# A hybrid encoder layer on one core: selection a block behind its queries, a deeper weight ring for the first tile, smaller gate blocks

## The chip, the core and the metric

The kernel runs on one core of a Trainium2 chip. TensorE (PE) multiplies, VectorE (DVE) and ScalarE (ACT) do elementwise work, GpSimd (POOL) issues the indirect DMAs that gather rows by index, and SyncE (SP) issues nearly all other DMAs, in the order in which they stand in its program. Every engine runs its own instructions in order; what is behind a waiting instruction waits too. The metric is the time of one execution in device microseconds.

## What is computed

One layer over 512 tokens of width 2048, all in float32: a normed projection, retention and dilated attention ("mixers"), their merge into the residual stream, and a product-key expert layer (PEER). The last part of the reference, which the change touches, is

```python
merged = sigmoid(gate_ret) * ret + sigmoid(gate_att) * att
x = x + merged @ w_out[l]
h2 = rms_norm(x, ffn_norm_g[l])
q = (h2 @ w_query).reshape(B, S, 8, 256)              # 8 heads
s1 = einsum('bshd,hkd->bshk', q[..., :128], sub_keys[:, 0])   # 128 keys each
s2 = einsum('bshd,hkd->bshk', q[..., 128:], sub_keys[:, 1])
v1, i1 = top_k(s1, 16); v2, i2 = top_k(s2, 16)
best, pos = top_k(v1[..., :, None] + v2[..., None, :], 16)    # over 256 pairs
experts = e1 * 128 + e2;  gates = softmax(best)
a   = gelu(h2 . u[experts]) * gates                   # 16384 experts, 8 x 16 per token
out = x + sum(a * v[experts])
```

## The kernel before

The 512 tokens are four tiles of 128. Tile 0 goes through the whole front alone, then tiles 1 to 3 together; the functions `mixers`, `merge` and `routing` are called once for each of these two stages (T = 1 and T = 3).

Every weight matrix comes through `load_w`: 512 KB pieces (`wraw`) are loaded by SP, ACT rounds each to `whi`, DVE takes the rest as `wlo` (L131), and PE uses both (L146 to L148). These buffers are a ring, opened by `weight_pool(raw, parts)`: raw pieces and parts that can be held at a time. It is (4, 4) from the start to the end of tile 0's routing, (3, 2) in the second `mixers`, (4, 3) in the second `merge` and `routing`.

`merge` multiplies by `w_ret_out` and `w_attn_out`, then `w_out`; the sum with x is kept in `x1`, stored to DRAM (`x1D`), squared for the norm on ACT (into `xr`), scaled in place by its norm and transposed. `routing` runs over four blocks c of 512 query columns: it multiplies (8 pieces of `w_query`), transposes the queries (L648) and multiplies with the keys `skT` (L653); then DVE picks the top 16 of all scores (L520 to L524, L668 to L710), 114 instructions for one block at T = 3. The keys come as 4 DMAs and are transposed on PE (L724). In the first stage four gemms of gates (`fillers`) run beside the four query gemms.

Tiles 0 and 1 get their experts by gathers: 256 each, one 1 MB row set for every (token column, expert) of u and then of v, issued by POOL (L756) and used on DVE (L765 for u, L774 for v). `tick(anchor, rate)` hangs `rate` gathers on a DVE instruction of other work. Tiles 2 and 3 get theirs densely: `expert_in(n)` multiplies the tokens with u of 128 experts (48 matmuls of 256 columns, L854 to L856; two `ur` loads, two `uh` on ACT, two `ul` on DVE), and `expert_out(g, i)` multiplies the gated results with v (L980 to L982, two loads `vr`, two `vl` on DVE). Their gates lie in a table in DRAM, `GD`, that is made in between: for 8 tokens at a time (an iteration; 32 of them) DVE makes one-hot rows (L912, L913, L922), ACT scales them (L920), PE multiplies them (L924), ACT copies the result to `Gs` (L926); a finished block of `Gs` (TB = 64 tokens, 4 MB) is stored to `GD`.

The order in the second stage: `routing` calls `begin_dense` behind its last query block, which runs the first NFIRST = 11 `expert_in`; behind the selection its results are transposed (hkT), written to DRAM and read back; then the 32 iterations with 12 more `expert_in` and one gather each; then the dense loop: 16 groups of 8 `expert_out` steps. The first three groups tick 0.7 gathers a step (`early_rate`), and two of them have no `expert_in` beside them; the gathers that are left are spread over the 96 steps of the next twelve groups. The program order on each engine is not that of the source: a scheduler places the instructions.

Of the kernel before, what the change touches and what calls it, by code (L numbers as in the profile page):

```python
# [10 lines left out]
F32 = mybir.dt.float32  # L11
BF16 = mybir.dt.bfloat16
F32R = mybir.dt.float32r
U32 = mybir.dt.uint32
I32 = mybir.dt.int32
AF = mybir.ActivationFunctionType
ALU = mybir.AluOpType
AX = mybir.AxisListType

P = 128  # L20
# [6 lines left out]
H = 8  # L27
# [37 lines left out]
def hybrid_layer(ctx, tc, I, out, dbg=None):  # L65
    nc = tc.nc
# [33 lines left out]
    ident = const.tile([P, P], F32, name="ident")  # L100
# [3 lines left out]
    def bank(name, pool=None):  # L104
        return (pool or psB).tile([P, 512], F32, name=name, tag="bank")
# [49 lines left out]
    with tc.tile_pool(name="x0", bufs=1) as x0:  # L155
# [22 lines left out]
        for k in range(KT):  # L178
            ps = bank("xT")
# [360 lines left out]
    def merge(part, mg, pieces):  # L540
# [63 lines left out]
        for c in range(4):  # L604
            cs = slice(c * 512, (c + 1) * 512)
            ps = gemm((I["w_out"][0], c * 512, tiles(mT)))[0]
            for t in range(T):
                xr = mg.tile([P, 512], F32, name="xr", tag="xr", bufs=3)
                nc.sync.dma_start(xr, x4[t0 + t][:, cs])
                nc.vector.tensor_add(x1[t][:, cs], ps[t], xr)  # L610
                nc.sync.dma_start(x1D[t0 + t][:, cs], x1[t][:, cs])
                nc.scalar.activation(xr, x1[t][:, cs], AF.Square, accum_out=ss4[:, t, c:c + 1])
        fg = mg.tile([P, KT], F32, name="ffng")
        nc.sync.dma_start(fg, I["ffn_norm_g"][0].rearrange("(k p) -> p k", p=P))
        for t in range(T):
# [17 lines left out]
    def routing(T, rt, skT, tab, tiles2, before_last=None):  # L633

        N2 = 2 * T
        gates, e1, e2 = [rt.tile([P, T, 8, 16], F32, name=n, bufs=1) for n in ("gates", "e1", "e2")]
        for c in range(4):
            ps = paired((I["peer_w_query"][0], c * 512, tiles2))
            qn = rt.tile([P, T, 512], F32, name="qn", bufs=2)
            for t in range(T):  # L640
                nc.scalar.copy(qn[:, t], ps[t])
            v12 = rt.tile([P, T, 2, 2, 16], F32, name="v12")
            i12 = rt.tile([P, T, 2, 2, 16], U32, name="i12")
            scs = []
            for i in range(4):
                pt = bank("qT")
                for t in range(T):
                    nc.tensor.transpose(pt[:, t * P:(t + 1) * P], qn[:, t, i * P:(i + 1) * P], ident)  # L648
                qT = rt.tile([P, T * P], F32, name="qTs", bufs=2)
                nc.scalar.copy(qT, pt[:, :T * P])  # L650
                ss = bank("s12")
                for t in range(T):
                    nc.tensor.matmul(ss[:, t * P:(t + 1) * P], qT[:, t * P:(t + 1) * P], skT[:, 4 * c + i],  # L653
                                     start=True, stop=True)
                sc = rt.tile([P, T * P], F32, name="s12s", bufs=4)
                nc.scalar.copy(sc, ss[:, :T * P])
                scs.append(sc)
            if c == 3 and before_last:
                before_last()
            for i in range(4):  # L660
                for t in range(T):
                    scr = rt.tile([P, P], F32, name="scr")
# [14 lines left out]
            for a in range(N2):  # L677
# [32 lines left out]
            nc.vector.tensor_mul(gates.rearrange("p t (c u) k -> p t c u k", c=4)[:, :, c],  # L710
                                 ex.rearrange("p (t u) k -> p t u k", t=T),
                                 sm.rearrange("p (t u) -> p t u", t=T)[:, :, :, None].to_broadcast([P, T, 2, 16]))
        return e1, e2, gates

    def routing_tables(rt):
        tab = rt.tile([P, 3, 16], F32, name="tab", bufs=1)
        nc.sync.dma_start(tab.rearrange("p a b -> p (a b)"), bcast(I["c_rank"], 48))
        skT = rt.tile([P, 16, P], F32, name="skT", bufs=1)
        for q4 in range(4):
            sk = rt.tile([P, 4, P], F32, name="sk", bufs=1)  # L720
            nc.sync.dma_start(sk, I["peer_sub_keys"][0].rearrange("h s k d -> k (h s) d")[:, 4 * q4:4 * q4 + 4])
            ps = bank("skT")
            for i in range(4):
                nc.tensor.transpose(ps[:, i * P:(i + 1) * P], sk[:, i], ident)  # L724
            nc.scalar.copy(skT[:, 4 * q4:4 * q4 + 4].rearrange("p a b -> p (a b)"), ps)
        return skT, tab


# [6 lines left out]
    def unit(t, e1, e2, gates, h2row):  # L735

        u = Unit()
        u.t = t
        u.eid = ga.tile([P, P], I32, name=f"eid{t}")
        u.gate = ga.tile([P, P], F32, name=f"gate{t}")  # L740
        ef = ga.tile([P, P], F32, name="ef", tag="ef")
        nc.vector.scalar_tensor_tensor(ef, flat(e1), float(P), flat(e2), op0=ALU.mult, op1=ALU.add)
        nc.vector.tensor_copy(u.eid, ef)  # L743
        nc.vector.tensor_copy(u.gate, flat(gates))
        u.h2 = h2row
        gstate["todo"] += [(u, s) for s in range(2 * P)]
        return u
# [40 lines left out]
    h2gD = dram.tile([P, D], F32, name="h2gD")  # L788
    mixers(0, True)
    wk_ctx.close()  # L790
    ga = ctx.enter_context(tc.tile_pool(name="ga", bufs=1, reuse_waits="tile"))
    with tc.tile_pool(name="mgA", bufs=1, reuse_waits="tile") as mg, \
            tc.tile_pool(name="rtA", bufs=2, reuse_waits="tile") as rt, \
            tc.tile_pool(name="flA", bufs=2, reuse_waits="tile") as fl:
# [11 lines left out]
        unit(0, e1[:, 0], e2[:, 0], gates[:, 0], h2gD)  # L806


    weight_pool(3, 2)
    mode["tick"] = lambda a: tick(a, 0.85)  # L810
    mixers(1, False)
# [2 lines left out]

    TG = 2
    ND = TG * P
    TB = 64
    NB = ND // TB
    NE = 2
    NV = 8  # L820
    NGRP = P // NV
    NPRE = 24
    NFIRST = 11
    NLAST = 1
    right = ctx.enter_context(ExitStack())
    pools = {}
# [68 lines left out]
    with tc.tile_pool(name="gb", bufs=1, reuse_waits="tile") as gb:  # L895
# [6 lines left out]
        for blk in range(NB):  # L902
            for n in range(*[NFIRST + (NPRE - NLAST - NFIRST) * (blk + i) // NB for i in (0, 1)]):
                expert_in(n)
            Gs = gb.tile([P, P, TB], F32, name="Gs")
            for o in range(TB // OB):
                t0 = blk * TB + o * OB
                cols = lambda v: v[:, t0:t0 + OB, None].to_broadcast([P, OB, P])
# [5 lines left out]
                for q in range(OB // 4):  # L914
# [9 lines left out]
                        nc.tensor.matmul(ps[:, i * P:(i + 1) * P], oh2[:, j], oh1[:, j], start=True, stop=True)  # L924
                    j0 = o * OB + 4 * q
                    nc.scalar.copy(Gs[:, :, j0:j0 + 4], ps.rearrange("p (t e) -> p e t", t=4))  # L926
                tick(last, 1.0)
            nc.sync.dma_start(GD[blk], Gs)
        for n in range(NPRE - NLAST, NPRE):
            expert_in(n)  # L930
# [7 lines left out]

    W = {}

    def gate_tile(m):
        Gt = d2.tile([P, NB, NE * TB], F32, name="Gt")
        nc.sync.dma_start(Gt, GD[:, :, NE * m:NE * (m + 1), :].rearrange("b p e t -> p b (e t)"))
        return Gt

    def weigh(m, Gt):
        ge = A_out.pop(m)
        gv = ge.rearrange("p j (b t) -> p b j t", t=TB)
        nc.vector.tensor_mul(gv, gv, Gt.rearrange("p b (j t) -> p b j t", t=TB))
        wh = d2.tile([P, NE, ND], F32R, name="wh", bufs=7)  # L950
        wl = d2.tile([P, NE, ND], F32R, name="wl", bufs=7)
        nc.scalar.copy(wh, ge)
        nc.vector.tensor_sub(wl, ge, wh.bitcast(F32))
        W[m] = (wh, wl)

    G0 = NPRE // NV
    early_rate = 0.7
    left_steps = [(NGRP - 1 - G0) * 8]

    def expert_out(g, i):  # L960
# [36 lines left out]
    for g in range(NGRP + 1):  # L997
        for q in range(NV):
            n = NV * g + q
            if n < P:  # L1000
                if n % NE == 0:
                    Gt = gate_tile(n // NE)
                if n >= NPRE:
                    expert_in(n)
                if n % NE == NE - 1:
                    weigh(n // NE, Gt)
            if g > 0:
                expert_out(g - 1, q)
# [8 lines left out]
def laid_out(inputs):  # L1017
    host = {n: np.ascontiguousarray(inputs[n]) for n in _INS}
    u = host["peer_u"].reshape(P, P, KT, P)
    host["u_feat"] = np.ascontiguousarray(u.transpose(0, 3, 2, 1)).reshape(P, P, KT * P)  # L1020
    host.update(shape_constants())
    return host

# [16 lines left out]
```

## Time and profile before

| | us |
|---|---|
| median of 3 runs | 4591.96 (4589.6 to 4595.62) |
| the profiled execution | 4602.08 |
| its span, first to last instruction | 4600.3 |
| PE busy in the span | 4211.8 (92%) |
| DVE busy | 3439.3 (75%) |
| ACT busy | 1917.0 (42%) |

The profiled execution is 10 us above the median, and 2 us of it lie outside its span. Busy PE time holds waits for weights inside a group of matmuls only in part, so a stage is read by its window: how long it lasts, how much of it PE and DVE are busy, which clock TensorE was granted (1.00 is full), and the share of the 16 DMA engines that was in use.

### The profile page before, as it was taken

The numbers are of one execution on the slowest core, as the hardware profiler recorded it, in microseconds if no ns is written. First come the engines' busy times: TensorE is split into PE (matmuls) and PEld (weight loads), VectorE is DVE, ScalarE is ACT, GpSimd is POOL, SyncE is SP. The second block draws the span as 40 slices with busy tenths as digits, with TensorE's granted clock in tenths as the row PEclk, the third lists the DMA queues.
The fourth block names the chain that finished last, engine by engine and source line by source line (L and its number), as shares of the span: only waits on it lengthen the run. The fifth ranks groups of instructions, "written<-read, shape, count | busy, mean of one in ns | idle before, by whom it ended". The sixth has DMA issues, their size and how long they took to land.

```text
span 4600.3 us, 57918 instructions
## 1 busy us (share of the span) xinstructions
PE 4211.8 (92%) x21638; PEld 3524.4 (77%) x21638; DVE 3439.3 (75%) x4495; ACT 1917.0 (42%) x2674; POOL 795.5 (17%) x516
## 2 busy tenths in 40 slices
PE   8999998988998999989979977886799999999999
PEld 6878776765776778767758866786689998899997
DVE  7454554546566878677678878888779998999997
ACT  6444555545442323443432333344434443344443
POOL 0000000000002112222122221012112332344332
PEclk9999999999999999999989998998899999999999
DMA  7666675758658889888899885267889999999997
GB/s 241 226 219 218 215 243 178 244 193 287 224 160 303 323 290 331 313 305 320 300 346 373 340 323 202 92 236 292 318 302 363 397 400 391 401 400 402 405 403 293
DMA packets 510171, 1358.78 MB, mean 295 GB/s; under 512 B 49216, under 2 KB 129088, under 8 KB 440768
## 3 DMA queue, kind: packets, MB, share of 16 engines
q1 hardware_dynamic: 432800, 816.00, 50.9%
q0 software_dynamic: 73728, 536.90, 29.7%
q8 instruction: 170, 2.79, 0.2%
q10 hardware_dynamic: 3360, 2.17, 0.2%
q14 instruction: 113, 0.93, 0.1%
HBM read 1290.05 MB, written 64.88 MB: 295 GB/s over the span
## 4 chain that ended last, share of the span: by engine, by line
PE 50%; DMA 18%; DVE 13%; issue 13%; ACT 3%; POOL 2%; SPq 0%; ACTq 0%; DVEq 0%; POOLq 0%
PE gB L147 9%; PE gB L148 9%; PE gB L146 9%; PE psy L981 3%; PE psy L982 3%; PE psy L980 3%; PE psa L856 3%; PE psa L854 3%; PE psa L855 3%; DMA gr<-in_peer_v,eid 3%; DMA ur<-in_u_feat 3%; DMA wraw<-in_w_in 2%; POOL gr L756 2%; DVE wlo L131 2%; DMA vr<-in_peer_v 2%
## 5 line engine op out<-in xcount | busy, mean ns | idle before, releaser
L131 DVE TENSOR_TENSOR wlo<-wraw,whi 128x1024 fp32r<-128x1024 f32 x752 | 917.2, 1223 | 650.6 <-ACT whi L130 636.0
L130 ACT CAST whi<-wraw 128x1024 fp32r<-128x1024 f32 x752 | 789.4, 1051 | 1227.7 <-PE gB L148 913.6
L756 POOL DMA_INDIRECT gr<-in_peer_u,eid x256 | 362.9, 1418 | 2752.8 <-DVE eid L743 1535.1
L774 DVE SCALAR_TENSOR_TENSOR accg<-gr,wg,accg 128x2048 f32<-128x2048 f32 x256 | 600.5, 2346 | 50.6 <-DMA gr<-in_peer_v,eid 38.5
L765 DVE SCALAR_TENSOR_TENSOR gr<-gr,hrow 128x2048 f32<-128x2048 f32 x256 | 583.8, 2284 | 45.7 <-DMA gr<-in_peer_u,eid 44.2
L854 PE MATMUL psa<-rh,uh 128*128 128x256 f32 x2048 | 582.1, 284 | 29.6 <-ACT uh L839 29.6
L756 POOL DMA_INDIRECT gr<-in_peer_v,eid x256 | 432.4, 1689 | 994.8 <-DVE accg L774 929.1
L856 PE MATMUL psa<-rh,ul 128*128 128x256 f32 x2048 | 581.8, 284 | 9.8 <-DVE ul L840 9.8
L855 PE MATMUL psa<-rl,uh 128*128 128x256 f32 x2048 | 580.0, 283 | 0.0
L839 ACT CAST uh<-ur 128x1024 fp32r<-128x1024 f32 x256 | 268.9, 1051 | 479.0 <-DMA ur<-in_u_feat 381.1
L981 PE MATMUL psy<-vl,wh 128*128 128x512 f32 x1024 | 405.1, 396 | 19.7 <-DVE vl L974 19.5
L854 PEld LDWEIGHTS psa<-rh,uh 128*128 128x128 f32 x2048 | 390.9, 191 | 34.7 <-ACT uh L839 30.5
L980 PE MATMUL psy<-vh,wh 128*128 128x512 f32 x1024 | 402.5, 393 | 6.0 <-ACT vh L973 5.9
L982 PE MATMUL psy<-vh,wl 128*128 128x512 f32 x1024 | 400.7, 391 | 0.0
L855 PEld LDWEIGHTS psa<-rl,uh 128*128 128x128 f32 x2048 | 397.6, 194 | 4.0
L856 PEld LDWEIGHTS psa<-rh,ul 128*128 128x128 f32 x2048 | 390.7, 191 | 12.2 <-DVE ul L840 12.0
L973 ACT CAST vh<-vr 128x1024 fp32r<-128x1024 f32 x256 | 267.9, 1050 | 300.6 <-DMA vr<-in_peer_v 164.5
L974 DVE TENSOR_TENSOR vl<-vr,vh 128x1024 fp32r<-128x1024 f32 x256 | 310.4, 1220 | 76.8 <-ACT vh L973 76.4
L147 PE MATMUL gB<-wlo,rh 128*128 128x512 f32 x768 | 316.3, 412 | 52.3 <-DVE wlo L131 52.0
L840 DVE TENSOR_TENSOR ul<-ur,uh 128x1024 fp32r<-128x1024 f32 x256 | 311.2, 1218 | 57.5 <-ACT uh L839 56.3
L146 PE MATMUL gB<-whi,rh 128*128 128x512 f32 x768 | 309.2, 406 | 31.5 <-ACT rh L570 22.7
L148 PE MATMUL gB<-whi,rl 128*128 128x512 f32 x768 | 311.0, 405 | 0.3 <-DVE rl L571 0.2
(467 smaller groups left out, 7957.5 us busy)
## 6 DMA issues: line engine op xcount, KB each, us to landing
wraw<-in_w_in SPq DMA_DIRECT2D x528, 512.0 KB, 5.0
ur<-in_u_feat SPq DMA_DIRECT2D x256, 512.0 KB, 9.6
vr<-in_peer_v SPq DMA_DIRECT2D x256, 512.0 KB, 9.9
wraw<-in_w_ret_out SPq DMA_DIRECT2D x64, 512.0 KB, 6.1
wraw<-in_w_out SPq DMA_DIRECT2D x64, 512.0 KB, 5.8
wraw<-in_peer_w_query SPq DMA_DIRECT2D x64, 512.0 KB, 4.9
wraw<-in_w_attn_out SPq DMA_DIRECT2D x32, 512.0 KB, 6.8
GD<-Gs SPq DMA_DIRECT2D x4, 4096.0 KB, 14.6
```

Source lines behind the costliest of these rows:

```text
L130: nc.scalar.copy(whi, raw)
L131: low = nc.vector.tensor_sub(wlo, raw, whi.bitcast(F32))
L146: nc.tensor.matmul(ps[t], ah(k), whi[:, j], start=first, stop=False)
L147: nc.tensor.matmul(ps[t], ah(k), wlo[:, j], start=False, stop=False)
L148: nc.tensor.matmul(ps[t], al(k), whi[:, j], start=False, stop=last)
L756: nc.gpsimd.indirect_dma_start(out=r, out_offset=None, in_=pu if s < P else pv_, in_offset=bass.IndirectOffsetOnAxis(ap=u.eid[:, s % P:s % ...
L765: nc.vector.scalar_tensor_tensor(r, r, 1.0, u.hrow, op0=ALU.mult, op1=ALU.mult, accum_out=u.ag[:, s:s + 1])
L774: nc.vector.scalar_tensor_tensor(u.acc, r, u.wg[:, s - P:s - P + 1], u.acc, op0=ALU.mult, op1=ALU.add)
L854: nc.tensor.matmul(psa[:, j], uh[:, cs], chi[k], start=k == 0, stop=False)
L855: nc.tensor.matmul(psa[:, j], uh[:, cs], clo[k], start=False, stop=False)
L856: nc.tensor.matmul(psa[:, j], ul[:, cs], chi[k], start=False, stop=k == KT - 1)
L981: nc.tensor.matmul(ps[:, t], wh[:, j, ts_], vl[:, j], start=False, stop=False)
```

## The change

Six things change.

1. `weight_pool(7, 6)` is opened for `merge` and `routing` of tile 0; the buffers of gathered rows (pool `ga`) are allocated behind that stage, and a small pool `ids` holds the expert numbers and gates.
2. In `merge` the sum goes into `xr`, which is stored; ACT squares it (into `x1`) and then copies it to `x1`. That is 16 more ACT copies of 128x512 in the whole kernel.
3. The keys are laid out on the host, and come as one 1 MB DMA without transposes.
4. In `routing` the selection of block c stands behind the queries of block c + 1; `begin_dense` therefore stands ahead of the last two selections. The score buffers are 8 in place of 4.
5. `GD` is made in 8 blocks of 32 tokens (2 MB) with two `Gs` buffers, and read 4 experts at a time in place of 2.
6. NFIRST is 16 in place of 11 (so 7 `expert_in` in place of 12 beside the iterations), the iterations tick 0.6 gathers in place of 1, and `early_rate` is 1.1 in place of 0.7.

```diff
@@ merge
-                nc.vector.tensor_add(x1[t][:, cs], ps[t], xr)
-                nc.sync.dma_start(x1D[t0 + t][:, cs], x1[t][:, cs])
-                nc.scalar.activation(xr, x1[t][:, cs], AF.Square, accum_out=ss4[:, t, c:c + 1])
+                nc.vector.tensor_add(xr, ps[t], xr)
+                nc.sync.dma_start(x1D[t0 + t][:, cs], xr)
+                nc.scalar.activation(x1[t][:, cs], xr, AF.Square, accum_out=ss4[:, t, c:c + 1])
+                nc.scalar.copy(x1[t][:, cs], xr)
@@ routing
-        for c in range(4):
+        def queries(c):
+
...
-                sc = rt.tile([P, T * P], F32, name="s12s", bufs=4)
+                sc = rt.tile([P, T * P], F32, name="s12s", bufs=8)
                 nc.scalar.copy(sc, ss[:, :T * P])
                 scs.append(sc)
-            if c == 3 and before_last:
-                before_last()
+            return scs
+
+        def select(c, scs):
...
+        found = {}
+        for c in range(4):
+            found[c] = queries(c)
+            if c == 3 and before_last:
+                before_last()
+            if c > 0:
+                select(c - 1, found.pop(c - 1))
+        select(3, found.pop(3))
         return e1, e2, gates
@@ routing_tables
-        for q4 in range(4):
-            sk = rt.tile([P, 4, P], F32, name="sk", bufs=1)
-            nc.sync.dma_start(sk, I["peer_sub_keys"][0].rearrange("h s k d -> k (h s) d")[:, 4 * q4:4 * q4 + 4])
-            ps = bank("skT")
-            for i in range(4):
-                nc.tensor.transpose(ps[:, i * P:(i + 1) * P], sk[:, i], ident)
-            nc.scalar.copy(skT[:, 4 * q4:4 * q4 + 4].rearrange("p a b -> p (a b)"), ps)
+        nc.sync.dma_start(skT, I["key_feat"].rearrange("d (a k) -> d a k", a=16))
@@ hybrid_layer
-    ga = ctx.enter_context(tc.tile_pool(name="ga", bufs=1, reuse_waits="tile"))
+    ids = ctx.enter_context(tc.tile_pool(name="ids", bufs=1, reuse_waits="tile"))
+    weight_pool(7, 6)
...
+    ga = ctx.enter_context(tc.tile_pool(name="ga", bufs=1, reuse_waits="tile"))
     weight_pool(3, 2)
...
-    TB = 64
+    TB = 32
...
-    NFIRST = 11
+    NFIRST = 16
...
-            Gs = gb.tile([P, P, TB], F32, name="Gs")
+            Gs = gb.tile([P, P, TB], F32, name="Gs", bufs=2)
...
-                tick(last, 1.0)
+                tick(last, 0.6)
...
-    early_rate = 0.7
+    early_rate = 1.1
```

Two places show how instructions move. The first is SP's row of DMAs at the border between the first `mixers` and the first `merge`: `sg_gr<-tm` is the last store of `mixers`, which waits for its last matmuls; `wraw<-in_w_ret_out` are the first weights of `merge`, `stg` its staged inputs. Before:

```order
185 L127 DMA wraw<-in_w_in 128x2x512
186 L127 DMA wraw<-in_w_ret_out 128x2x512 x7
187 L516 DMA sg_gr_353<-tm_7513 128x1536
188 L127 DMA wraw<-in_w_ret_out 128x2x512
189 L717 DMA tab<-in_c_rank 128x48
190 L721 DMA sk<-in_peer_sub_keys 128x4x128
191 L556 DMA stg<-retD_348 128x128 x4
192 L582 DMA sg<-sg_gr_352 128x512
```

and now:

```order
185 L127 DMA wraw<-in_w_in 128x2x512
186 L516 DMA sg_gr_353<-tm_7513 128x1536
187 L729 DMA tab<-in_c_rank 128x48
188 L731 DMA skT<-in_key_feat 128x2048
189 L556 DMA stg<-retD_348 128x128 x4
190 L127 DMA wraw<-in_w_ret_out 128x2x512
191 L556 DMA stg<-retD_348 128x128 x4
192 L127 DMA wraw<-in_w_ret_out 128x2x512 x2
```

Seven loads of `w_ret_out` that stood ahead of the last store now stand behind it, between the staged inputs.

The second is DVE's row in the second `routing` at the border between query blocks 0 and 1: `wlo` is the split of the next weights, `accg` a gather's use, the rest is selection. Before:

```order
1945 L521 MAX_INDEX pos<-best,cand 128x8
1946 L524 MAX_INDEX pos<-best,scr_20855 128x8
1947 L522 MATCH_REPLACE scr_20861<-best,cand 128x50
1948 L683 COPY di<-i12f 128x6
1949 L684 TENSOR_TENSOR di<-i12f 128x6x15
1950 L523 MAX best<-scr_20861 128x8
1951 L131 TENSOR_TENSOR wlo<-wraw,whi 128x1024
1952 L524 MAX_INDEX pos<-best,scr_20861 128x8
```

and now:

```order
1880 L521 MAX_INDEX i_20976<-v_20975,s12s 128x8
1881 L524 MAX_INDEX i_20976<-v_20975,scr 128x8
1882 L131 TENSOR_TENSOR wlo<-wraw,whi 128x1024
1883 L779 SCALAR_TENSOR_TENSOR accg<-gr,wg,accg 128x2048
1884 L522 MATCH_REPLACE scr<-v_20975,s12s 128x128
1885 L520 MAX v_20975<-s12s 128x8
1886 L131 TENSOR_TENSOR wlo<-wraw,whi 128x1024
1887 L779 SCALAR_TENSOR_TENSOR accg<-gr,wg,accg 128x2048
1888 L523 MAX v_20975<-scr 128x8
1889 L521 MAX_INDEX i_20976<-v_20975,s12s 128x8
1890 L524 MAX_INDEX i_20976<-v_20975,scr 128x8
1891 L522 MATCH_REPLACE scr<-v_20975,s12s 128x128
1892 L131 TENSOR_TENSOR wlo<-wraw,whi 128x1024
```

The split ahead of row 1951 is row 1853: before, 99 instructions of the selection (rows 1854 to 1950, with repeats) stood as one block between two splits of the next query block's weights; now 32 of it stand ahead of the next split and the rest is shared out, the two longest blocks without a split being 54 and 67, and 85 behind the last query block. On PE the row of `expert_in` matmuls between the last scores and the transposes hkT grows from 11 to 16 experts.

## Rows read from the trace of the kernel before

**Rows 1.** The page: busy us, share of the span and instructions.

```profile
PE 4211.8 (92%) x21638; PEld 3524.4 (77%) x21638; DVE 3439.3 (75%) x4495; ACT 1917.0 (42%) x2674; POOL 795.5 (17%) x516
```

**Rows 2.** Windows: busy us (instructions) by engine, clock, DMA share, GB/s.

```profile
core 0: us, PE busy (x) PEld busy (x) DVE busy (x) ACT busy (x) POOL busy (x), PEclk, DMA share, GB/s
1028.00:1155.00 127.00, 106.98 (x403) 71.97 (x404) 88.21 (x94) 71.36 (x86) 0.00 (x0) 0.99 0.84 284
...
2752.00:2965.00 213.00, 170.57 (x760) 134.59 (x759) 180.32 (x592) 63.95 (x107) 17.35 (x12) 0.90 0.39 140
2815.00:2965.00 150.00, 113.98 (x489) 89.58 (x487) 134.03 (x476) 36.95 (x54) 9.85 (x6) 0.89 0.32 112
2965.00:3046.00 81.00, 78.10 (x661) 77.10 (x660) 65.88 (x189) 39.01 (x46) 1.68 (x1) 0.98 0.58 196
3046.00:3262.00 216.00, 149.91 (x1081) 143.09 (x1081) 184.38 (x275) 100.55 (x220) 52.35 (x31) 0.83 0.73 282
3284.00:3405.00 121.00, 110.05 (x470) 86.83 (x469) 97.69 (x95) 47.26 (x50) 17.26 (x13) 0.98 0.88 314
3405.00:4485.00 1080.00, 1070.39 (x6909) 975.35 (x6908) 1002.36 (x815) 441.76 (x480) 379.07 (x199) 1.00 1.01 392
```

**Rows 3.** DMA of 1028:1155, the first tile's merge.

```profile
wraw<-in_w_out SPq DMA_DIRECT2D x32, 512.0 KB, 5.2
```

**Rows 4.** Waits of ACT in 1028:1155: total us, times, longest.

```profile
ACT whi L130 <- DMA wraw<-in_w_out: 26.1, 26, 3.6
ACT whi L130 <- DMA wraw<-in_w_ret_out: 17.7, 15, 2.6
```

**Rows 5.** SP's timeline around the border of first mixers and merge.

```profile
958.38 24.85 SPq L127 DMA_DIRECT2D wraw<-in_w_ret_out  x7
985.23 0.34 SPq L516 DMA_DIRECT2D sg_gr<-tm  x1
...
988.82 1.93 SPq L556 DMA_DIRECT2D stg<-retD  x4
```

**Rows 6.** DVE's timeline between the second merge and its transposes.

```profile
2738.94 0.28 DVE L619 RECIPROCAL ssx<-ssx 128x1 f32<-128x1 f32 x3
2744.03 1.29 DVE L623 TENSOR_SCALAR x<-x,ssx 128x2048 f32<-128x2048 f32 x1 [4.81 <-DMA x1D<-x]
```

**Rows 7.** Waits of PE in 2752:2965, the second query blocks.

```profile
PE gB L147 <- DVE wlo L131: 33.7, 6, 9.3
PE skT L724 <- DMA sk<-in_peer_sub_keys: 6.4, 3, 4.4
```

**Rows 8.** Groups of DVE instructions in 2815:2965.

```profile
L131 DVE TENSOR_TENSOR wlo<-wraw,whi 128x1024 fp32r<-128x1024 f32 x21 | 25.4, 1211 | 5.4 <-ACT whi L130 5.4
L774 DVE SCALAR_TENSOR_TENSOR accg<-gr,wg,accg 128x2048 f32<-128x2048 f32 x7 | 16.4, 2348 | 1.6 <-DMA gr<-in_peer_v,eid 1.6
```

**Rows 9.** Groups of PE in 3000:3025, where only experts run.

```profile
L854 PE MATMUL psa<-rh,uh 128*128 128x256 f32 x70 | 20.0, 286 | 0.0
```

**Rows 10.** PE's and DVE's timeline: the transposes hkT, the first iteration.

```profile
3032.33 0.60 PE L888 MATMUL hkT<-ident,e 128*128 128x128 f32 x4
...
3046.04 1.23 DVE L912 TENSOR_TENSOR oh<-hkT,iota 128x1024 f32<-128x1024 f32 x1 [2.18 <-DMA hkT<-hk_T]
```

**Rows 11.** Groups of DVE in 3046:3262, the iterations.

```profile
L765 DVE SCALAR_TENSOR_TENSOR gr<-gr,hrow 128x2048 f32<-128x2048 f32 x29 | 66.1, 2283 | 6.4 <-DMA gr<-in_peer_u,eid 5.1 <-DMA hrow<-h2D 1.3
...
L840 DVE TENSOR_TENSOR ul<-ur,uh 128x1024 fp32r<-128x1024 f32 x23 | 27.4, 1219 | 19.8 <-ACT uh L839 19.8
```

**Rows 12.** DVE's timeline: iterations without a gather, then with one.

```profile
3061.13 1.22 DVE L912 TENSOR_TENSOR oh<-hkT,iota 128x1024 f32<-128x1024 f32 x1
...
3063.89 1.22 DVE L912 TENSOR_TENSOR oh<-hkT,iota 128x1024 f32<-128x1024 f32 x1
...
3093.01 1.21 DVE L912 TENSOR_TENSOR oh<-hkT,iota 128x1024 f32<-128x1024 f32 x1
...
3097.99 1.22 DVE L912 TENSOR_TENSOR oh<-hkT,iota 128x1024 f32<-128x1024 f32 x1
```

More of the change, by code (lines that the diff above doesn't have):

```diff
@@ L641, in routing @@
                 nc.scalar.copy(qn[:, t], ps[t])
-            v12 = rt.tile([P, T, 2, 2, 16], F32, name="v12")
-            i12 = rt.tile([P, T, 2, 2, 16], U32, name="i12")
             scs = []
@@ L654, in routing @@
                                      start=True, stop=True)
-                sc = rt.tile([P, T * P], F32, name="s12s", bufs=4)
+                sc = rt.tile([P, T * P], F32, name="s12s", bufs=8)
                 nc.scalar.copy(sc, ss[:, :T * P])
                 scs.append(sc)
-            if c == 3 and before_last:
-                before_last()
+            return scs
+        def select(c, scs):
+            v12 = rt.tile([P, T, 2, 2, 16], F32, name="v12")
+            i12 = rt.tile([P, T, 2, 2, 16], U32, name="i12")
             for i in range(4):
@@ L738, in unit @@
         u.t = t
[L739 to L743, printed above, removed]
+        u.eid = ids.tile([P, P], I32, name=f"eid{t}")
+        u.gate = ids.tile([P, P], F32, name=f"gate{t}")
+        nc.vector.scalar_tensor_tensor(u.gate, flat(e1), float(P), flat(e2), op0=ALU.mult, op1=ALU.add)
+        nc.vector.tensor_copy(u.eid, u.gate)
         nc.vector.tensor_copy(u.gate, flat(gates))
@@ L939, in hybrid_layer, with gate_tile @@
     W = {}
-    def gate_tile(m):
-        Gt = d2.tile([P, NB, NE * TB], F32, name="Gt")
-        nc.sync.dma_start(Gt, GD[:, :, NE * m:NE * (m + 1), :].rearrange("b p e t -> p b (e t)"))
+    NG = 4
+    def gate_tile(i):
+        Gt = d2.tile([P, NB, NG * TB], F32, name="Gt")
+        nc.sync.dma_start(Gt, GD[:, :, NG * i:NG * (i + 1), :].rearrange("b p e t -> p b (e t)"))
         return Gt
@@ L948, in weigh @@
         gv = ge.rearrange("p j (b t) -> p b j t", t=TB)
-        nc.vector.tensor_mul(gv, gv, Gt.rearrange("p b (j t) -> p b j t", t=TB))
+        nc.vector.tensor_mul(gv, gv, Gt.rearrange("p b (j t) -> p b j t", t=TB)[:, :, m % 2 * NE:(m % 2 + 1) * NE])
         wh = d2.tile([P, NE, ND], F32R, name="wh", bufs=7)
@@ L1000, in hybrid_layer @@
             if n < P:
-                if n % NE == 0:
-                    Gt = gate_tile(n // NE)
+                if n % NG == 0:
+                    Gt = gate_tile(n // NG)
                 if n >= NPRE:
@@ L1020, in laid_out @@
     host["u_feat"] = np.ascontiguousarray(u.transpose(0, 3, 2, 1)).reshape(P, P, KT * P)
+    keys = host.pop("peer_sub_keys").reshape(2 * H, P, P)
+    host["key_feat"] = np.ascontiguousarray(keys.transpose(2, 0, 1)).reshape(P, 2 * H * P)
     host.update(shape_constants())
```

## Prediction

> **What bounds the kernel now.** I read the page first, then the windows, then inside each window what PE waits for. PE is busy 92% of the span and DVE 75% [rows 1], but the average hides three kinds of stage [rows 2]. In the dense loop (3405 to 4485) PE is busy 1070 of 1080 us at full clock, DVE 1002 us, and the DMA engines are in use all the time (1.01, 392 GB/s): it is set by PE, with little room on DVE and none to be seen on DMA. In the second query blocks (2752 to 2965) and the iterations (3046 to 3262) PE is busy 171 of 213 and 150 of 216 us, at a clock of 0.90 and 0.83, while DVE is busy 180 and 184: DVE is in the lead. In the first tile's merge (1028 to 1155) the DMA share is 0.84 and neither engine is full.
>
> **First tile's merge, edit 1.** ACT waits for weights there, 26.1 and 17.7 us for the two big matrices [rows 4]. A piece takes 5.2 us to land [rows 3], then a cast and a split, and with four buffers the queue runs dry in between. Seven buffers can take the DMA share from 0.84 towards 1. At 0.96 the 127 us become 127 x 0.84 / 0.96 = 111: 16 us. Bounds: nothing, and 127 x 0.16 = 20 us.
> The Trainium skill (DMA: Bandwidth & Descriptors, section Bandwidth) says that for transfers between HBM and SBUF a core's HBM share of about 358 GB/s binds, not the engines' own rate. By that rule the 284 GB/s here could rise by a quarter, an estimate of 26 us. The dense loop's 392 GB/s [rows 2] already lies above that figure, so the share, not the rate, is what I go by.
> Against it: seven `w_ret_out` loads, which SP issued from 958.4 on under the end of `mixers`, now stand behind its last store and between the staged inputs. The first staged input is issued at 988.8 [rows 5] either way, and the first block needs all of them, so I cost the late start at nothing; with no cover it is 7 pieces x 127 us x 0.84 / 70 pieces, about 11 us (the window moves 284 GB/s x 127 us = 36 MB, some 70 pieces). So -16, bounds -20 and +11.
>
> **The sum in `xr`, edit 2.** In the second merge the reciprocals of the norm are ready at 2738.9, but the scaling of x1 in place starts at 2744.0, after 4.81 us of waiting for the store `x1D` out of the same rows [rows 6]. Now the store reads `xr`, and this wait goes. The copies are on ACT, which is idle there but for the squares; the last ones sit in the chain, some 0.6 us each by the like square. I take -4 in all. What is late next: `xr` is reloaded only when its store has landed, and SP stands in front of the next `w_out` loads meanwhile; that is up to 5 us, under four pieces already loaded. Bounds -6 and +4.
>
> **Keys, edit 3.** In the second routing PE waits 6.4 us for `sk` [rows 7], and 16 transposes go. -8, bounds -9 and -4; the one DMA lands ahead of need, since the first scores come only behind 8 pieces. In the first stage this is part of the late start above.
>
> **Selection a block later, edit 4.** PE waits 33.7 us for `wlo` in the second query blocks, 9.3 at most [rows 7]. From 2815 to 2965 DVE is busy 134.0 us [rows 2], of which splits 25.4 and gathers 16.4 [rows 8]; the rest, 92 us, is three selections of 114 instructions: 31 us each, 0.27 an instruction. The ring holds three split pieces, each 18 matmuls. Experts alone run 210 matmuls of 256 columns in 25 us [rows 9], 0.119 us each; 18 of 512 columns are then 4.3 us, and three pieces cover 12.9 us. 99 selection instructions (26.7 us) overrun that by 14; the measured 33.7 us over three borders is 11 each, so the reckoning is some 30% high. Now the blocks are 32, 54 and 67: 8.6, 14.6 and 18.1 us, an overrun of 0, 2 and 5, and 85 (23 us) ahead of the first expert's `ul`, which the last scores hide in part: 6. So 13 us of waits in place of 34: -21, bounds -34 (all gone) and -5.
>
> **Five experts more ahead of the iterations, edit 6.** 210 expert matmuls in 25 us [rows 9] are 5.7 us for 48; five are 28.6 us. DVE has in that stretch 95 + 114 selection instructions (56 us) and 37 splits of 1.22 (45 us), 101 us against PE's 16 x 5.7 = 91, less the 17 us that lie ahead; so the two are level, and I add 2 us: +31, bounds +24 and +40. The way from hkT (3032.3) to the first one-hot row (3046.0) [rows 10] stays.
>
> **Iterations, edits 5 and 6.** An iteration without a gather takes 3063.89 - 3061.13 = 2.76 us of DVE, with one 3097.99 - 3093.01 = 4.98, so a gather costs 2.22 [rows 12]. 32 x 2.76 = 88.3; now 0.6 x 32 = 19 gathers, 42.2; the splits of 5.5 experts, 11 x 1.22 = 13.4: 144 us. Before the same sum is 88.3 + 31 x 2.22 + 23 x 1.22 = 185 [rows 11, 12] against a window of 216 [rows 2], the difference being waits: 19.8 for `uh` and 6.4 for rows of the gather [rows 11], and the rest for hkT. The waits for `uh` come where three splits stand in one clump and PE must free the buffers; the clumps are now of two and half as many, so 18 us in all: 162 us. -54, bounds -72 (no waits) and -40 (the waits of now). Two `Gs` buffers take away ACT's wait for the store; the first `Gt` waits for a last store of 2 MB in place of 4: -4, bounds -7 and 0.
>
> **Where the gathers go.** 13 leave the iterations. The 24 early steps take 26 in place of 17, and the 96 later ones 210 in place of 207. Early (3284 to 3405) DVE is busy 97.7 of 121 us and DMA 0.88 [rows 2]; 7 gathers more in that window are 16 us of DVE and 7 MB, which brings both to about 0.94 and 1.0: +5, bounds 0 and +17. Later 3.4 gathers are 8 us of DVE over 1080 and 3.4 MB, 8.6 us at 392 GB/s if DMA is the bound: +3, bounds 0 and +9.
>
> **Sum.** -16 - 4 - 8 - 21 + 31 - 54 - 4 + 5 + 3 = -68. Against the profiled execution's 4602 that is 4534; against the median of the runs, 10 lower, 4524. That DVE can do it: from 2752 to 3262 it is busy 431 of 510 us [rows 2]; without 13 gathers 401 of some 450, 89%, which the dense loop's 93% shows to be possible.
>
> **Rivals.**
> The iterations don't follow DVE. Once it has less to do, the chain one-hot, scaling on ACT, matmul, copy on ACT sets the pace. ACT is busy 101 of 216 us there, and iterations of 2.76 us have run back to back, which speaks against it. If the stage only falls by 20 us, the sum is -34: 4558.
> The gathers meet a full DMA. Where the early and the late steps are both bound by it, 13 MB cost 13 / 0.392 = 33 us in place of 8: -43, 4549. The share of 1.01 speaks for it, PE's 1070 of 1080 against.
> The deeper ring changes nothing and starts late (+11 in place of -16): -41, 4551.
> Slower: the dense loop tips. If DMA need passes what it can give, at some 400 GB/s, PE waits a little at each step, and its clock falls as it does wherever it waits (0.89 from 2815 to 2965, 0.98 early [rows 2]). At 0.93 the 1080 us become 1161: +81 + 9, in all some +19: 4611. It decides from about 2% more traffic a step; the change brings under 1%.
> The skill (Perfetto Trace Analysis, section Roofline) puts the ceiling of a core alone at about 435 GB/s for its 16 DMA engines; by that there would be room and this rival falls away. The trace shows a share of 1.01 at 392 GB/s, which says there is none.
>
> **Chances and range.** As summed 0.62; iterations 0.13; full DMA 0.10; ring 0.06; slower 0.05; no change to speak of, several of the gains at their lower bounds, 0.04. The likeliest gives 4524. The range goes down to 4480, where the waits of the iterations and of the queries are gone (-18 and -13, and some of the early cost), and up to 4568, past the three smaller gains. A measurement of this kernel tells about 0.2%, 9 us, from no change. Faster 0.91, same 0.04, slower 0.05.
>
> **What would show it.** Right: the first merge's DMA share above 0.9; no wait for `x1D` ahead of the scaling; waits of PE for `wlo` under 20 us in the second query blocks; the first one-hot row near 3020 to 3045 but the last iteration below 3215; gathers on DVE 19 in the iterations; the dense loop as long as before. Wrong: a DMA share that stays at 0.84 with more buffers; long rows of ACT or PE waits between iterations; PE waits for `vl` or `uh` in the dense loop, with a clock below 1.00.

## The result, and the profile after

The changed kernel takes 4529.87 us (median of 4 runs, 4524.72 to 4537.17), the kernel before 4593.79 in the same comparison: ratio 0.986, 95% interval 0.9839 to 0.9881. The forecast was 4524, 4480 to 4568. The total came within 6 us of the forecast, but not all of its terms did: two gains were larger than forecast, and one cost was seven times its size.

The page of the changed kernel:

```profile
span 4535.4 us, 57812 instructions
PE 4210.1 (93%) x21606; PEld 3528.5 (78%) x21606; DVE 3435.4 (76%) x4495; ACT 1921.0 (42%) x2682; POOL 813.9 (18%) x516
```

The engines do nearly the same work as in [rows 1]: PE is busy 1.7 us less and DVE 3.9 us less, so the time gained was waiting. Windows of the changed kernel, with the same work in them as the windows of [rows 2] (first tile's merge, query blocks, their second part, from the first expert to the first one-hot row, iterations, early steps, the dense loop, and the late steps alone, from the fourth group's first `expert_out` matmul to the last group's):

```profile
core 0: us, PE busy (x) PEld busy (x) DVE busy (x) ACT busy (x) POOL busy (x), PEclk, DMA share, GB/s
1027.00:1139.00 112.00, 101.60 (x410) 75.63 (x409) 87.57 (x94) 70.90 (x88) 0.00 (x0) 0.97 0.93 323
...
2717.00:2896.00 179.00, 162.54 (x744) 131.13 (x742) 166.10 (x571) 61.50 (x103) 16.32 (x12) 0.94 0.49 180
...
2775.00:2896.00 121.00, 107.52 (x485) 86.54 (x483) 118.94 (x470) 36.21 (x53) 6.89 (x6) 0.95 0.39 138
2896.00:3005.00 109.00, 106.23 (x884) 104.77 (x884) 90.61 (x219) 49.61 (x58) 1.94 (x1) 0.98 0.56 192
3005.00:3168.00 163.00, 119.80 (x873) 114.30 (x873) 147.07 (x242) 90.33 (x209) 35.62 (x19) 0.88 0.74 275
3188.00:3316.00 128.00, 114.96 (x459) 88.92 (x459) 108.26 (x104) 46.87 (x50) 27.88 (x19) 0.93 0.94 341
3316.00:4420.00 1104.00, 1081.42 (x6919) 979.71 (x6918) 1014.64 (x827) 443.86 (x482) 388.65 (x205) 0.99 1.01 390
3381.00:4479.00 1098.00, 1075.35 (x6869) 973.41 (x6867) 1015.39 (x815) 438.83 (x477) 402.60 (x210) 0.99 1.01 391
```

The late steps of the kernel before:

```profile
3469.00:4544.00 1075.00, 1065.30 (x6868) 969.97 (x6866) 1009.63 (x809) 437.71 (x477) 395.98 (x207) 1.00 1.02 397
```

The first merge went from 127 to 112 us with the DMA share at 0.93; the query blocks from 213 to 179, DVE now busy 93% of them; the iterations from 216 to 163. The dense loop, forecast nearly as long as before, went from 1080 to 1104. In its late steps PE runs as many matmuls as before, but it is busy 10 us more, at a granted clock of 0.99 in place of 1.00, and idle 13 us more.

One execution of each is thin evidence for stages, so both kernels were profiled twice. This table is worked out from the start times of matmuls and one-hot rows (end of one stage to the end of the next; each cell has the two executions):

| stage | before | after | change of means | forecast |
|---|---|---|---|---|
| start to last matmul of the first mixers | 984.2, 981.0 | 976.7, 978.6 | -5.0 | 0 |
| to the first `w_ret_out` matmul | 9.7, 10.6 | 12.9, 13.2 | +2.9 | 0 (+11) |
| first merge | 161.5, 163.7 | 149.9, 147.8 | -13.8 | -16 |
| first routing, second mixers, second merge | 1573.3, 1568.0 | 1562.9, 1564.7 | -6.9 | 0 |
| second merge's end to the first query matmul | 23.1, 19.9 | 14.7, 14.7 | -6.8 | -4 |
| query blocks, to the first expert matmul | 213.0, 215.1 | 179.1, 173.9 | -37.6 | -29 |
| experts ahead, to hkT | 67.5, 68.6 | 96.2, 95.4 | +27.8 | +31 |
| hkT to the first one-hot row | 13.7, 13.5 | 13.1, 12.1 | -1.0 | 0 |
| iterations, first to last one-hot row | 204.6, 205.1 | 150.6, 145.9 | -56.6 | -54 |
| to the first `expert_out` matmul | 30.4, 32.1 | 29.0, 29.3 | -2.1 | -4 |
| early dense steps | 188.0, 190.1 | 196.3, 193.4 | +5.8 | +5 |
| late dense steps | 1074.5, 1075.2 | 1097.5, 1097.4 | +22.6 | +3 |
| last group | 51.2, 51.2 | 51.0, 48.6 | -1.4 | 0 |

The sum is -72, and the medians give -64: the two profiled executions of the kernel before lie some 8 us above its median, those of the changed kernel average its median. The first and fourth rows, 12 us together, hold mostly work that no edit touches. Among the ten profiles below and above in which the first routing and the second mixers have the same code, these two alone range over 18 us (1178 to 1196), so the 12 us are not explained.

### The profile page after: what moved, and what is told of

It reads as the page before. It is cut to its first block, busy times and chain, and to the rows that moved or that the text cites. A ratio compares the mean times of both kernels' runs of the same rounds, so it can differ in the third digit from the quotient of the medians.

```text
span 4535.4 us, 57812 instructions
## 1 busy us (share of the span) xinstructions
PE 4210.1 (93%) x21606; PEld 3528.5 (78%) x21606; DVE 3435.4 (76%) x4495; ACT 1921.0 (42%) x2682; POOL 813.9 (18%) x516
## 4 chain that ended last, share of the span: by engine, by line
PE 48%; DMA 19%; DVE 14%; issue 12%; ACT 4%; POOL 2%; SPq 0%; DVEq 0%; ACTq 0%; POOLq 0%
PE gB L147 10%; PE gB L148 10%; PE gB L146 10%; DMA vr<-in_peer_v 4%; DMA gr<-in_peer_v,eid 3%; PE psy L990 3%; PE psy L991 3%; PE psa L863 3%; PE psa L861 3%; PE psy L989 2%; PE psa L862 2%; DMA ur<-in_u_feat 2%; DMA wraw<-in_w_in 2%; DVE wlo L131 2%; POOL gr L761 2%
## 5 line engine op out<-in xcount | busy, mean ns | idle before, releaser
L779 DVE SCALAR_TENSOR_TENSOR accg<-gr,wg,accg 128x2048 f32<-128x2048 f32 x256 | 600.2, 2344 | 52.9 <-DMA gr<-in_peer_v,eid 37.6
L761 POOL DMA_INDIRECT gr<-in_peer_v,eid x256 | 444.2, 1735 | 945.8 <-DVE accg L779 842.8
```

Source lines behind the costliest of these rows:

```text
L761: nc.gpsimd.indirect_dma_start(out=r, out_offset=None, in_=pu if s < P else pv_, in_offset=bass.IndirectOffsetOnAxis(ap=u.eid[:, s % P:s % ...
L779: nc.vector.scalar_tensor_tensor(u.acc, r, u.wg[:, s - P:s - P + 1], u.acc, op0=ALU.mult, op1=ALU.add)
```

## Experiments

Two runs repeat the two kernels, and two (fewer gathers still, two gathers a step) go further than the change; all others are the changed kernel with something undone. Each is timed against the kernel before on its chip, and the ratio is the time over that kernel's. "The changed kernel" in what follows has the ratios 0.986 and 0.9866 in its two measurements, and 4530 us.

### The changed kernel again

> The changed kernel once more, as the base of the other runs. In its first profile the stage from the first to the last expert_out matmul (called the dense stage) takes 1344.8 us, 31 us more than before the change, where the prediction had 8. Theory A (DMA is the bound there, and each of the 12 to 13 gathers moved into it costs its 1 MB at 392 GB/s, 2.6 us): the dense stage again within 8 us of 1345. Theory C (the excess is scatter of one execution): a dense stage under 1330. Time 4530 either way, within 8.

Measured: 4529.83 us, ratio 0.9866 (0.9847 to 0.9884). Dense stage 1339.4 us, late steps 1097.4. Theory C is out: the longer late steps are real.

### The kernel before again

> The kernel before once more, for its stages. The late dense steps (from the fourth group's first expert_out matmul to the last group's) took 1075 us in its first profile, against 1091 to 1098 in three kernels with 207 or 210 gathers there. Scatter: this time 1085 to 1100. Something of the change that slows these steps by 15 to 23 us, apart from the number of gathers: 1070 to 1080 again. First mixers again within 8 us of 984.

Measured: 4601.56 us. Late steps 1075.2, first mixers 981.0. Both kernels repeat their late steps within 1 us. The 23 us belong to the change.

### Both rates back

```diff
-                tick(last, 0.6)
+                tick(last, 1.0)
-    early_rate = 1.1
+    early_rate = 0.7
```

> Only the two rates go back: 1.0 gather an iteration in place of 0.6 and 0.7 an early dense step in place of 1.1; 16 experts stay ahead. 13 gathers leave the dense stage and go back to the iterations. Theory A (full DMA in the dense stage): iterations (first to last one-hot row) 151 + 13 x 2.2 = 179 us, dense stage 1345 - 31 = 1314 us: time within 6 of the changed kernel's. Theory B (the prediction's terms: 29 us on DVE against 8 in the dense stage): iterations 179, dense stage 1337: 20 us slower than the changed kernel.

Measured: 4551.26 us, 0.9904 (0.9888 to 0.9919): 21 us slower than the changed kernel, as theory B has it. Its windows (iterations, early steps, late steps, in two answers):

```profile
core 0: us, PE busy (x) PEld busy (x) DVE busy (x) ACT busy (x) POOL busy (x), PEclk, DMA share, GB/s
3001.00:3184.00 183.00, 119.80 (x844) 114.08 (x845) 173.18 (x266) 90.55 (x209) 52.54 (x31) 0.84 0.84 312
3203.00:3389.00 186.00, 177.89 (x889) 148.68 (x889) 145.49 (x138) 75.12 (x81) 28.33 (x18) 0.96 0.87 309
...
3389.00:4487.00 1098.00, 1073.71 (x6865) 972.37 (x6864) 1007.92 (x809) 437.56 (x477) 391.97 (x207) 1.00 1.01 388
```

The iterations take 23 us more than the mean of the two profiles after, the early steps 9 less. The late steps have 207 gathers again, as before the change, and still take 1098 us. So the number of gathers alone is not what lengthened them: they move as many bytes as before in more time, at 388 GB/s in place of 397. Of the 13 gathers that left the dense stage, 9 left the early steps and 3 the late ones.

### Fewer gathers still in the iterations

```diff
-                tick(last, 0.6)
+                tick(last, 0.2)
```

> Only the rate in the iterations changes, 0.2 in place of 0.6: 13 more gathers go into the 96 late dense steps (2.33 a step in place of 2.19). Theory A: iterations 151 - 29 = 122 us if DVE still sets their pace, dense stage 1345 + 13 x 2.6 = 1379: about 5 us slower than the changed kernel. Theory B (a gather in the dense stage costs some 0.6 us): dense stage 1353, 20 us faster than the changed kernel. A third way: the dense loop tips, PE loses clock at each wait, and the stage grows by over 50.

Measured: 4532.77 us, 0.9861 (0.9847 to 0.9876): the same as the changed kernel. Iterations and late steps:

```profile
3000.00:3131.00 131.00, 111.13 (x891) 107.34 (x892) 119.54 (x217) 89.52 (x210) 11.27 (x6) 0.96 0.67 251
...
3343.00:4476.00 1133.00, 1084.92 (x6869) 980.81 (x6867) 1044.41 (x841) 439.07 (x477) 394.66 (x223) 0.98 1.01 391
```

DVE still sets the pace of the iterations, which take 29 us less from first to last one-hot row than in the two profiles after, 2.3 a gather. But 13 gathers more in the late steps cost 35 us, 2.7 each, the price of theory A: at 391 GB/s a gather's 1 MB is 2.7 us. DVE's own work went up too, from 1015 to 1044 us, so this run does not separate a full DMA from a full DVE. PE's clock falls to 0.98; the stage does not tip.

### Gate table back

```diff
-    TB = 32
+    TB = 64
-            Gs = gb.tile([P, P, TB], F32, name="Gs", bufs=2)
+            Gs = gb.tile([P, P, TB], F32, name="Gs")
-    NG = 4
+    NG = 2
```

> Only the gate table goes back to 64 tokens a block, one Gs buffer, and a 256 KB gate tile for every 2 experts in place of 512 KB for 4. Theory A: the dense stage stays within 8 of 1345 us, and the time rises by 4 (0 to 7), the way from the last iteration to the first expert_out being longer. Theory D (the longer dense stage comes of the 512 KB gate tiles, which hold up the loads behind them): the dense stage falls by 15 to 23 us, and the kernel is some 15 us faster than the changed one.

Measured: 4527.43 us, 0.9857 (0.9842 to 0.9872): no difference. Late steps 1091.0; the way from the last iteration to `expert_out` 31.3 in place of 29.1. The late steps:

```profile
3378.00:4469.00 1091.00, 1072.19 (x6868) 975.22 (x6866) 1016.26 (x815) 440.06 (x476) 383.52 (x210) 0.99 1.01 394
```

Neither theory is met in full.

### The keys in the old input's place

```diff
-        nc.sync.dma_start(skT, I["key_feat"].rearrange("d (a k) -> d a k", a=16))
+        nc.sync.dma_start(skT, I["peer_sub_keys"].rearrange("d (a k) -> d a k", a=16))
...
-    host["key_feat"] = np.ascontiguousarray(keys.transpose(2, 0, 1)).reshape(P, 2 * H * P)
+    host["peer_sub_keys"] = np.ascontiguousarray(keys.transpose(2, 0, 1)).reshape(P, 2 * H * P)
```

> The changed kernel, instruction for instruction, but the laid-out keys come as the input peer_sub_keys, in its old place among the inputs, in place of a new input behind u_feat. If the place of the inputs in HBM is what lowers the late dense steps' transfers from 397 to 391 GB/s, these steps fall from 1097 to about 1077 us and the kernel is 20 us faster than the changed one. Otherwise nothing changes: within 5 us.

Measured: 4537.35 us, 0.9875 (0.9854 to 0.9896): no difference. Late steps 1089.5:

```profile
3388.00:4477.00 1089.00, 1070.69 (x6865) 973.12 (x6863) 1014.86 (x815) 439.80 (x476) 395.85 (x210) 1.00 1.01 394
```

That is a part of the 23 us at most. It may be none: the late steps of four kernels that differ from the changed one only ahead of them (the four runs behind the next) lie between 1090.9 and 1101.7.

### Rates, gate table and input place back together

The edits of the rates, the gate table and the keys' input, shown above, in one kernel.

> Of the changed kernel all that touches the dense stage goes back together but for the 16 experts ahead: both rates (1.0 and 0.7), gate blocks of 64 tokens with tiles for 2 experts, and the keys in the old input's place. If these three make the late dense steps longer, each by a part (alone they gave 1098, 1091 and 1090 against 1097), the late steps are 1075 to 1082. If it is the order that 16 experts and the later selections leave behind, they stay at 1088 to 1100. The time is that of the run with the rates back, 4551, less what the late steps give.

Measured: 4539.06 us, 0.9876 (0.9856 to 0.9897): no difference from the changed kernel that the time can tell, and 12 us less than with the rates alone back, where 25 were expected; the iterations took 179.0 us here and 171.3 there. Late steps 1073.0. Their window, and what PE waits for in it:

```profile
3403.00:4476.00 1073.00, 1066.46 (x6865) 972.45 (x6863) 1009.54 (x809) 441.56 (x477) 390.23 (x207) 1.00 1.02 397
```

```profile
PE psy L990 <- DVE vl L983: 3.5, 3, 2.7
PE psa L863 <- DVE ul L847: 3.0, 1, 3.0
```

The changed kernel, 3381 to 4479:

```profile
PE psy L990 <- DVE vl L983: 18.0, 14, 2.8
PE psa L863 <- DVE ul L847: 3.0, 1, 3.0
PE psy L989 <- ACT vh L982: 1.4, 1, 1.4
```

The kernel before, 3469 to 4544:

```profile
PE psy L981 <- DVE vl L974: 7.1, 8, 2.4
```

The late steps are back at the length that they had before, with 397 GB/s, and PE's waits for `vl` fall from 18.0 to 3.5 us. Sixteen experts ahead and the later selections are still in, so they alone are not the cause. Undoing the three together gave 24 us back; alone they gave 0, 6 and 8, of which the 6 and the 8 are no more than kernels differ that change nothing in these steps. This is one profile of one kernel; which of the three it takes is not shown.

### Ring back

```diff
-    ids = ctx.enter_context(tc.tile_pool(name="ids", bufs=1, reuse_waits="tile"))
-    weight_pool(7, 6)
+    ga = ctx.enter_context(tc.tile_pool(name="ga", bufs=1, reuse_waits="tile"))
+    ids = ga
...
-    ga = ctx.enter_context(tc.tile_pool(name="ga", bufs=1, reuse_waits="tile"))
```

> Edit 1 alone is undone: the ring stays (4, 4) through the first tile's merge and routing, and the gathers' buffers are allocated ahead of it. Theory of the prediction, as the first profile corrects it (the deeper ring starts some 7 us late and then gains 18): the first merge 10 us longer, the rest alike: 10 us slower than the changed kernel, 4540. Rival (the late start eats all, the shorter merge is the scatter of one execution or the single load of the keys): within 3 us of the changed kernel in this stage. Should the SBUF places of the gathers' buffers be what makes the late dense steps longer, these fall from 1097 to about 1077, and the kernel is 10 us faster instead.

Measured: 4549.86 us, 0.9907 (0.9887 to 0.9927): 20 us slower than the changed kernel. Border and merge, 992 to 1153, beside the changed kernel's 990 to 1139:

```profile
992.00:1153.00 161.00, 133.38 (x495) 89.98 (x496) 109.27 (x131) 90.42 (x125) 0.00 (x0) 0.97 0.81 269
```

```profile
990.00:1139.00 149.00, 129.76 (x493) 94.53 (x493) 111.03 (x131) 91.67 (x122) 0.00 (x0) 0.92 0.92 317
```

The first merge takes 160.8 us, 12 more, with the DMA share back at 0.81. In the eleven profiles with the deeper ring it takes 147 to 152. The border to the first `w_ret_out` matmul is 12.5 us here too, although SP's timeline has seven loads of `w_ret_out` ahead of the last store again, as [rows 5]:

```profile
953.99 24.85 SPq L127 DMA_DIRECT2D wraw<-in_w_ret_out  x7
980.83 0.34 SPq L516 DMA_DIRECT2D sg_gr<-tm  x1
```

So the 3 us that the border grew by are not those of the ring's late start. The keys' single 1 MB load now stands ahead of the staged inputs, in this kernel too, and ACT's longest wait for such an input there is 8.8 us in the changed kernel and 10.2 here, in place of 7.2; that this is the reason was not tested. Late steps 1095.1: the place of the gathers' buffers is not their cause. The other 8 us of the 20 have no stage that stands out of the scatter.

### Selection back

```diff
-            if c > 0:
-                select(c - 1, found.pop(c - 1))
-        select(3, found.pop(3))
+            select(c, found.pop(c))
```

> Edit 4 alone is undone: each block's selection stands behind its own queries, with the first 16 experts ahead of the last selection only. Prediction: PE's waits for wlo in the second query blocks go from 9 back to 34 us, and the kernel is 21 (5 to 34) us slower than the changed one. Rival (PE's waits there were of the DMA order or of the keys, not of DVE's long blocks): the query blocks stay within 5 us of 130, and the time too.

Measured: 4558.54 us, 0.9911 (0.9893 to 0.9929): some 20 to 29 us slower than the changed kernel. PE's longest wait in the query blocks, then the same wait in the changed kernel:

```profile
PE gB L147 <- DVE wlo L131: 32.8, 6, 9.3
```

```profile
PE gB L147 <- DVE wlo L131: 9.1, 3, 3.5
```

From the first query matmul to the first expert's the stage takes 203.0 us, against 176.5 in the two profiles after: 26 us. Kernels with the later selection lie between 174 and 182 there, so the size is known to some 4 us. The kernel before has this selection too, with the old keys, and takes 214: 11 us are left for the keys.

### The sum back in x1

> Edit 2 alone is undone: the sum goes to x1 again, is stored from there and scaled in place. Prediction: DVE waits some 5 us for the store x1D ahead of the scaling in the second merge, and the stretch from the end of the second merge to the first query weights' matmuls, 76 to 83 us in the changed kernel, grows by 4 (to 6). Rival (the shorter stretch is the keys' alone): it stays at 80, within 2. The time tells either from the changed kernel's only beyond 9 us.

Measured: 4538.73 us, 0.9867 (0.9845 to 0.9889): no difference that the time can tell. DVE's timeline at the scaling:

```profile
2721.31 0.28 DVE L619 RECIPROCAL ssx<-ssx 128x1 f32<-128x1 f32 x3
2723.77 1.28 DVE L623 TENSOR_SCALAR x<-x,ssx 128x2048 f32<-128x2048 f32 x1 [2.17 <-DMA x1D<-x]
2731.20 1.29 DVE L623 TENSOR_SCALAR x<-x,ssx 128x2048 f32<-128x2048 f32 x1 [6.15 <-DMA wraw<-in_peer_w_query]
```

and in the changed kernel:

```profile
2712.95 0.28 DVE L620 RECIPROCAL ssx<-ssx 128x1 f32<-128x1 f32 x3
2713.14 2.48 DVE L624 TENSOR_SCALAR x<-x,ssx 128x2048 f32<-128x2048 f32 x2
```

The wait for the store is there again, and a second one that the page lays on a weight load ahead of the second tile. The stretch from the merge's last matmul to the first query matmul is 20.9 us in place of 14.7, so the shorter stretch is not the keys' alone. The query blocks behind it take 173.6 us, at the lower end of the 174 to 182 of the other kernels; how much of the 6 us reaches the total is not shown.

### Eleven experts ahead

```diff
-    NFIRST = 16
+    NFIRST = 11
```

> Only NFIRST goes back from 16 to 11: five experts stand beside the iterations again. By the prediction's terms the way from the first expert matmul to hkT shortens from 96 to 67 us, and the iterations grow by 10 splits of 1.22 and about 13 of waits, from 150 to 175: some 5 us faster than the changed kernel. By the run with both rates back (iterations 171 with 16 experts ahead and one gather each, 205 in the kernel before with 11) they grow by 33, to 183: 4 us slower. If 16 experts ahead are also what lengthens the late dense steps, these fall from 1097 to about 1080, and the kernel is some 15 us faster.

Measured: 4533.72 us, 0.9867 (0.9846 to 0.9889): the same. Experts ahead 70.0 us in place of 95.8, but hkT to the first one-hot row 20.2 in place of 12.6, iterations 158.3 in place of 148.2, and early steps 200.7 in place of 194.9. Late steps 1090.9. Five experts more ahead bring nothing by themselves once the iterations have fewer gathers.

### Two gathers a step

```diff
-    early_rate = 1.1
-    left_steps = [(NGRP - 1 - G0) * 8]
+    early_rate = 1.5
+    left_steps = [(NGRP - 1 - G0) * 8 + 4]
...
-        elif g < NGRP - 1:
+        elif g < NGRP - 1 or i < 4:
```

> A version meant to be faster: early_rate 1.5 in place of 1.1, and the last gathers spread over 100 steps in place of 96 (four steps of the last group, where the DMA share was 0.78). 200 gathers over 100 steps are 2 a step in place of 2.19. If a full DMA sets the late steps (13 gathers more cost 35 us there), they fall from 1097 to about 1073; the early steps grow by 8 to 12 with 10 gathers more at the 0.8 us that they cost there so far, the last group by 4: 5 to 12 us faster than the changed kernel. If the late steps don't follow (207 gathers took 1098), the early steps' cost is left: 12 us slower.

Measured: 4555.19 us, 0.9914 (0.9891 to 0.9937): 25 us slower than the changed kernel. Early steps, then late:

```profile
3191.00:3415.00 224.00, 188.74 (x886) 152.71 (x887) 181.54 (x172) 74.62 (x80) 66.66 (x35) 0.93 0.92 337
```

```profile
3416.00:4486.00 1070.00, 1064.22 (x6863) 970.90 (x6863) 982.28 (x793) 443.98 (x477) 351.46 (x193) 1.00 1.00 386
```

The late steps do fall, by 27 us for 17 gathers fewer, to where PE is busy 1064 of 1070. The DMA share is 1.00 even here, at 386 GB/s, where PE hardly waits. But the ten gathers more in the early steps cost 29 us, not 8 to 12, and the last group 8. No version tried is faster than the changed kernel by more than the measurement can tell.

## Why the prediction was right, and where not

**The deeper ring: right.** The share rose from 0.84 to 0.93, the merge lost 13.8 us, and undoing the edit gave 12 of them back; forecast -16. ACT's waits for weights in 1027:1139, 26.1 and 17.7 us in [rows 4], are now

```profile
ACT whi L130 <- DMA wraw<-in_w_out: 15.8, 17, 4.0
ACT whi L130 <- DMA wraw<-in_w_ret_out: 2.5, 8, 0.4
```

Its late start cost nothing, as forecast: the border is as long with four buffers.

**The sum in `xr`: right in mechanism and near in size.** The wait for `x1D` of [rows 6] went. It was worth 6 us at its place, where 4 were forecast; the time of the kernel cannot tell it.

**Keys and selection: right in mechanism, under-sized together.** PE's waits for `wlo` fell from 33.7 [rows 7] to 9.1, where 13 were forecast. Undoing the selection cost 26 us against the forecast 21, and 11 are left for the keys against 8; the latter is a difference between kernels, not a run of its own, and the scatter does not tell which of the two was under-sized. The forecast counted PE's waits alone; PE's busy time in these blocks fell as well, from 170.6 to 162.5 us, with the transposes of the keys gone and a granted clock of 0.94 in place of 0.90 [rows 2]. DVE's splits, selections and gathers now fill 119 of the last 121 us.

**Experts ahead and iterations: right.** +28 for +31 and -57 for -54. With the rates back the iterations took 171 and 179 us in place of 148: the rates give 23 to 31 of the 57, where 13 gathers of 2.22 us make 29. Of 31 gathers beside the iterations 19 are left, as forecast:

```profile
L770 DVE SCALAR_TENSOR_TENSOR gr<-gr,hrow 128x2048 f32<-128x2048 f32 x17 | 38.7, 2283 | 3.9 <-DMA hrow<-h2D 3.9
L779 DVE SCALAR_TENSOR_TENSOR accg<-gr,wg,accg 128x2048 f32<-128x2048 f32 x2 | 4.7, 2345 | 0.0
```

The rest, 26 to 34, came with five experts fewer beside the iterations while these had a gather each, about what the five cost ahead of them (28). With the new rates the five are worth only 10 us in the iterations, and 18 with the way from hkT. So what the experts are worth there depends on the rates. Moving the experts is neutral in the total, as its terms said (+31 against about 25), and the rates carried the gain.

**Where the gathers go: the step that failed.** "Later 3.4 gathers are 8 us of DVE over 1080 [...]: +3, bounds 0 and +9." Measured: +22.6, in both profiles of the changed kernel. The step took over the late steps of [rows 2] as they were and only added to them the work and the bytes of a few gathers. But PE did not keep its pace there: of the 23 us, 13 are idle time of PE, most of it waits for `vl` (18.0 us in place of 7.1), and 10 are a longer busy time at a clock of 0.99. Going back to 207 gathers with the rates changed none of this (1098 us), and undoing rates, gate tiles and input place together removed it. So the few gathers more are not the whole cause. Nor is their price the small one of the step: 13 more cost 35 us, and 17 fewer gave 27 back, until PE was all but never idle.

The size is near that of the rival of a full DMA (33 in place of 8, over early and late steps: 28 measured), and so is the price of the 13 gathers. That the DMA engines are what holds the late steps is still not shown. The rate in GB/s is bytes over the length of the stage and falls when the stage gets longer for any reason, the share was 1.00 also where PE hardly waited, and what PE waits for is a split on DVE.

The slower rival, in which PE waits a little at each step and its clock falls, is there in small: a clock of 0.99, and 0.98 with 13 gathers more, not the 0.93 that it was priced at. By the Trainium skill (Perfetto Trace Analysis, section Roofline), with about 435 GB/s for a core alone, there would have been room for the gathers; no late window here goes above 397, at a share of 1.01 or 1.02.

**Signs and luck.** Most of the signs of being right came. The first one-hot row stands at 3005 and 3000, earlier than the 3020 to 3045 named, because the stages ahead gained more. The dense loop is not as long as before, and a sign of being wrong came with it: PE's waits for `vl` at a clock below 1.00. That the total is within 6 us is in part luck: the late steps lost 20 us more than forecast, while the query blocks gained 9 more and stages that hardly change 12.

**Open:** which of the three edits, in which pair, lengthens the late steps, and whether DVE or the DMA engines hold them. Pairs were not run, nor the new rates with gate table and input place both undone, which might keep the iterations' gain and the 1073 us.

## What to carry to other kernels

Work that moves from a stage bound by one engine into a stage whose DMA share is already 1.0 is best priced at its bytes over the measured rate, unless a run shows less: here 2.7 us per 1 MB gather against 2.3 us on the engine it relieved, so that moving 13 more gained nothing. A long block of one engine's work between two splits that another engine waits for is worth spreading out: that, the ring and the rates were what cost 20 us or more to undo. Before reading a stage's difference of 10 us, profile both kernels twice, and others that leave the stage alone: the late steps of one kernel repeated within 1 us, but differed by 11 between kernels with the same code there, and the first routing and second mixers differed by 18.

## What was not expected of the hardware

At the same share (1.01 to 1.02) the 16 DMA engines moved 388 to 397 GB/s in the late steps of kernels with 207 or 210 gathers there; the median time from issue to landing was not longer where the rate was lower (`vr` 9.8 us in the changed kernel, 10.4 in the one before). With two gathers a step the share was 1.00 at 386 GB/s, while PE was busy 1064 of 1070 us. So a share of 1.0 says neither that the rate is the highest to be had nor that the stage waits for the DMA engines. Three changes that alone gave back 0, 6 and 8 us of these steps gave back 24 together.
